# Hybrid decoder trunk: other start addresses for the operands that TensorE reads

## The chip, the cores and the metric

The kernel runs on one core of a Trainium2 chip. The metric is the device time of one execution in microseconds. Before the change the median of 3 runs is 823.48 us (822.98 to 824.05).

## What is computed

The reference is a decoder trunk of two layers over 256 tokens of width 1024, all in float32. A layer is a SwiGLU feed-forward block (width 1408, half a step), a token-mixing block and a second feed-forward block:

```python
for l in range(DEPTH):                                             # DEPTH = 2
    x = x + 0.5 * _swiglu(_rms_norm(x, ffn1_norm[l]), ffn1_wi[l], ffn1_wo[l])
    u = _rms_norm(x, mix_norm[l])
    c = _split_cols(u @ w_in[l] + b_in[l])                         # 1024 x 6312
    y_sb = _stick_breaking_attention(...); y_ml = _mlstm(...); y_mla = _mla(...)
    g = sigmoid(c['gates'])                                        # three gates of 1024
    merged = g0*(y_sb @ w_up_sb[l]) + g1*(y_ml @ w_up_ml[l]) + g2*(y_mla @ w_up_mla[l])
    x = x + merged @ w_out[l]
    x = x + 0.5 * _swiglu(_rms_norm(x, ffn2_norm[l]), ffn2_wi[l], ffn2_wo[l])
```

Nearly all arithmetic is in products of the 256 tokens with weight matrices that stream once from HBM.

## The kernel before

Float32 precision is kept with two numbers of type float32r for each value, a high part and the rest. `mm3` (L604) makes each product of three matmuls: standing high by moving high, standing high by moving low, standing low by moving high. "Standing" is the operand that a weight load (LDWEIGHTS) puts into the array ahead of the matmul, 128 columns of 4 bytes, so 512 bytes of each partition; "moving" is the operand that then streams through, 256 to 512 columns, so 1024 to 2048 bytes. Each matmul has its own weight load, and the load for the next one runs beside the matmul.

In most products the weights stand and the activations move, 256 tokens at a time: the normed input `u` (L613), the hidden rows of the feed-forward blocks and the merged branches, in the buffers R1 to R4. Each k-slice is a row of 256 float32, 1024 bytes. A few products are turned round (`tok_units`, L712; the first columns of the mixing block, L952; the last output projection, L862): there the activations stand and the weights move.

A weight tile lands by DMA in a buffer `raw`; ScalarE makes its high part (`conv_hi`, L364), VectorE the rest (`conv_lo`, L374). The two parts go either into a ring of five buffers each (`whi`, `wlo`) or into two of eight slots of 4 KB (`g4_0` to `g4_7`). The slots also hold the gates and the outputs of the three branches, and these outputs move against `whi` and `wlo` in the up projections (L1092).

Start addresses are set by `LAYOUT` (L210): before anything else the constructor takes these buffers in this order, each group padded to a multiple of 256 bytes. The activations begin 12 floats further (`SHIFT`, L209, in `moving`, L250), and so do weights that move (L366). In the built program this gives, modulo 256 bytes: activations at 48, ring weights that stand at 0, ring weights that move at 48, all slots at 0. Every row and every 128-column piece is a multiple of 256 bytes long, except the 424-column rows, so these numbers hold for each operand. In the text a pair (48, 0) means moving at 48 and the next standing operand at 0.

The order of the work is not fixed by hand: while the program is built, `Flow` (L84) keeps estimated times, and `drive` (L416) issues matmuls, conversions and side work by them. `Flow` notes when a piece of 256 bytes of a tile is written (`pieces`, L109), counted from the start of its tile.

Of the kernel before, what the change touches and what calls it, by code (L numbers as in the profile page):

```python
# [11 lines left out]
F32R = mybir.dt.float32r  # L12
# [6 lines left out]
P = 128  # L19
S = 256  # L20
# [52 lines left out]
class WTile:  # L73


    def __init__(self, srcs, shape, cls):
        self.srcs, self.shape, self.cls = srcs, shape, cls
        self.n = int(np.prod(shape))
        self.first = self.last = self.hi = self.lo = None
        self.not_before = 0  # L80
        self.moves = False
# [121 lines left out]
class Trunk:  # L203
# [2 lines left out]
    SLACK, NEAR, BACK = 0.1, 6, 1.5  # L206


    FIRST, LINE, SHIFT = 16512, 256, 12  # L209
    LAYOUT = (("u", 4112, 1), ("R2", 2064, 1), ("R1", 2072, 1), ("R3", 784, 1), ("R4", 784, 1),  # L210
              ("whi", 1088, 5), ("wlo", 1088, 5), *((f"g4_{i}", 1024, 1) for i in range(8)))

    def __init__(self, ctx, tc, a, out):
        self.tc, self.a, self.out = tc, a, out
        self.nc = Core(tc.nc)
        self.flow = self.nc.flow
        pool = lambda name, **k: ctx.enter_context(tc.tile_pool(name=name, bufs=1, **k))
        self.cp = self.wp = self.ap = pool("all")
        self.mm = pool("mm", space=bass.MemoryType.PSUM)
        self.at = pool("at", space=bass.MemoryType.PSUM)  # L220
        self.n = 0
        self.units, self.tiles, self.hooks = [], [], {}
        self.sides = []
        self.ring = {}
        self.slots = {"ps": [None] * 4, "mm": [None] * 2, "t384": [None] * 6, "g4": [None] * 8}
        self.last = {k: list(v) for k, v in self.slots.items()}
        end = self.FIRST
        for tag, n, bufs in self.LAYOUT:
            pad = -end % self.LINE
            if pad:  # L230
                self.ap.tile([P, pad // 4], F32, tag=f"before_{tag}", name=f"before_{tag}", bufs=1)
            self.tile(self.ap, [P, n], tag, bufs, F32R)
            end += pad + -(-n // 8) * 32 * bufs
# [12 lines left out]

    def sb(self, shape, tag, bufs=1, dt=F32):
        return self.tile(self.ap, shape, tag, bufs, dt)

    def moving(self, shape, tag):  # L250

        n = int(np.prod(shape[1:]))
        t = self.sb([P, self.SHIFT + n], tag, dt=F32R)[:, self.SHIFT:]
        return t.rearrange("p (a b c) -> p a b c", a=shape[1], b=shape[2]) if len(shape) == 4 else t.rearrange("p (a c) -> p a c", a=shape[1])

    def s2k(self, shape):
        return self.sb(shape, "s2k", 5)
# [105 lines left out]

    def conv_hi(self, w):  # L364
        if w.slot == "m":
            o = self.SHIFT if w.moves else 0  # L366
            w.fh, w.fl = (self.tile(self.wp, [P, 1088], s, self.RING, F32R)[:, o:o + 1024] for s in ("whi", "wlo"))
        else:
            w.fh, w.fl = self.g4([P, 1024], F32R), self.g4([P, 1024], F32R)
        view = lambda t: t[:, :w.n].rearrange("p (a b) -> p a b", a=w.shape[0])  # L370
        w.hi, w.lo = view(w.fh), view(w.fl)
        self.nc.scalar.copy(w.fh[:, :w.n], w.raw[:, :w.n])
# [237 lines left out]


    def new_u(self, N):
        u = self.moving([P, 2, 8, S], "u")  # L613
        N["h"], N["l"] = u[:, 0], u[:, 1]
        N["n"] = N["m"] = 0

# [130 lines left out]
    def plan_ffn(self, l, wi, wo, U, N):  # L747
        a, nc = self.a, self.nc
        H = {"k": set()}

        def hT(k):
            if k not in H["k"]:
                return None
            return (H["ah"][:, k], H["al"][:, k]) if k < 8 else (H["bh"][:, k - 8], H["bl"][:, k - 8])

        def alloc():
            if len(H) == 1:
                H["ah"], H["al"] = self.moving([P, 8, S], "R1"), self.moving([P, 8, S], "R2")
                H["bh"], H["bl"] = self.moving([P, 3, S], "R3"), self.moving([P, 3, S], "R4")

        def dst(k0, n):
            hi, lo, k = (H["ah"], H["al"], k0) if k0 < 8 else (H["bh"], H["bl"], k0 - 8)
            H["k"].update(range(k0, k0 + n))
            return hi[:, k:k + n], lo[:, k:k + n]

        wv = a[wi][l].rearrange("(k p) (g f) -> p k g f", p=P, g=2)

        def tiles(c0, w, cuts):
            return [WTile([(wv[:, k0:k1, g, c0:c0 + w], (0, k1 - k0, g * w, (g + 1) * w)) for g in range(2)],
                          (k1 - k0, 2 * w), "mx") for k0, k1 in zip(cuts, cuts[1:])]  # L770

        def side_feat(box, k0, n):
            v = box["v"]
            alloc()
            yield lambda: "row" in U,
            yield "v", U["row"], v
            h = self.s2k([P, 2, 256])[:, :n]
            nc.vector.tensor_tensor(h, v[:, 0:n, :], U["row"].unsqueeze(1).to_broadcast([P, n, S]), ALU.mult)
            yield "a", h
            nc.scalar.activation(h, h, AF.Silu)  # L780
            yield "v", h
            nc.vector.tensor_tensor(h, h, v[:, n:2 * n, :], ALU.mult)
            self.give(box["pp"])
            yield "a", h
            hi, lo = dst(k0, n)
            self.split(hi, lo, h)

        for c in range(5):
            box = {}
            cuts = (0, 1, 2, 4, 6, 8) if not self.units else (0, 2, 4, 6, 8)  # L790
            self.feat_units(tiles(256 * c, 256, cuts), 4, U, box,
                            lambda b=box, c=c: self.spawn(side_feat(b, 2 * c, 2)), key="n")
        box = {}
        self.feat_units(tiles(1280, 128, (0, 4, 8)), 2, U, box, lambda b=box: self.spawn(side_feat(b, 10, 1)), key="n")
        if N is None:
            self.plan_last(a[wo][l], 11, hT, U)
        else:
            self.plan_down(a[wo][l], 11, hT, N, U)
# [124 lines left out]
    def plan_mix(self, l, U, M, N):  # L923
        nc, a = self.nc, self.a
        col = lambda r: M["cols"][:, r:r + 1]
        wv = a["w_in"][l].rearrange("(k p) n -> p k n", p=P)
        b = a["b_in"][l]
# [158 lines left out]
        def up_units(q):  # L1086
# [5 lines left out]
            def part(w, j, k, kk, first, last):  # L1092

                if "p" not in box:
                    pp = self.big_ps()
                    box["p"] = [self.main_ps(), pp[:, 0, :], self.main_ps(), pp]
                y = M["y", j]
                for mi in range(2):
                    ms = slice(mi * P, (mi + 1) * P)
                    self.mm3(box["p"][j][:, mi * S:(mi + 1) * S], w.hi[:, kk, ms], w.lo[:, kk, ms], y[0][:, k], y[1][:, k],  # L1100
                             first, last, first=mi == 0)
                if last:
                    box["j"] = j
                    if j == 0:
                        self.spawn(merge())

            def merge():
                if q == 0:
                    M["mh"], M["ml"] = self.moving([P, 8, S], "R1"), self.moving([P, 8, S], "R2")
                    M["merged"] = 0  # L1110
                acc = None
                m0 = 2 * (q % 2)
                for j in (0, 1, 2):
                    yield lambda: box["j"] >= j,
                    yield "v", M["g", q // 2, j], box["p"][j]
                    o = self.s2k([P, 2, S])
                    nc.vector.scalar_tensor_tensor(o, M["g", q // 2, j][:, m0:m0 + 2, :], 1.0,
                                                   box["p"][j].rearrange("p (m c) -> p m c", m=2), ALU.add, ALU.mult)
                    if acc is None:
                        acc = o  # L1120
                    else:
                        nc.vector.tensor_tensor(acc, acc, o, ALU.add)
                self.give(box["p"][0], *box["p"][2:])
                if q % 2:
                    self.give(*[M["g", q // 2, j] for j in range(3)])
                yield "a", acc
                self.split(M["mh"][:, 2 * q:2 * q + 2], M["ml"][:, 2 * q:2 * q + 2], acc, 0.5)
                M["merged"] += 1
# [400 lines left out]
```

## Time and profile before

| | |
|---|---|
| median of 3 runs | 823.48 us (822.98 to 824.05) |
| profiled execution, its own time | 823.87 us |
| its span, first to last instruction | 822.1 us |
| TensorE busy | 814.6 us, 99% of the span, 6475 matmuls |
| weight loads busy | 788.0 us, 6475 loads |
| VectorE, ScalarE, GpSimd busy | 587.1, 455.4, 35.4 us |
| granted TensorE clock | 1.00 of 2.4 GHz over the span |

Busy time counts a matmul from its start to its modelled end, and matmuls overlap, so a busy share of 99% says that TensorE hardly ever waits, not how fast it goes. How fast it goes is read from starts: in the timeline, the difference between two start times divided by the number of matmuls in between is the interval that one matmul costs. All recorded instructions have line 189, the helper that records them, so groups go by tile names: `u` and `R` are activations, `whi` and `wlo` the ring, `g` the slots, `t` the small 1536-byte buffers. The first name after the arrow moves, the second stands; `at` and `mm` are PSUM buffers.

### The profile page before, as it was taken

The numbers are of one execution on the slowest core, as the hardware profiler recorded it, in microseconds if no ns is written. First come the engines' busy times: TensorE is split into PE (matmuls) and PEld (weight loads), VectorE is DVE, ScalarE is ACT, GpSimd is POOL, SyncE is SP. The second block draws the span as 40 slices with busy tenths as digits, with TensorE's granted clock in tenths as the row PEclk, the third lists the DMA queues.
The fourth block names the chain that finished last, engine by engine and source line by source line (L and its number), as shares of the span: only waits on it lengthen the run. The fifth ranks groups of instructions, "written<-read, shape, count | busy, mean of one in ns | idle before, by whom it ended". The sixth has DMA issues, their size and how long they took to land.

```text
span 822.1 us, 16189 instructions
## 1 busy us (share of the span) xinstructions
PE 814.6 (99%) x6475; PEld 788.0 (96%) x6475; DVE 587.1 (71%) x943; ACT 455.4 (55%) x724; POOL 35.4 (4%) x51
## 2 busy tenths in 40 slices
PE   8999999999999999999999999999999999999998
PEld 6999999899999999999999999998999999999996
DVE  5687878989667488755776567789967585886641
ACT  7456645658675546544554444665576845555430
POOL 0000000200200000000000000110003000000000
PEclk9999999999999999999999999999999999999999
DMA  8678834654264757865576554366543665587611
GB/s 257 197 226 253 266 110 137 202 156 122 85 205 153 233 167 219 258 191 168 155 228 204 179 166 141 105 207 182 157 119 112 200 183 183 179 250 218 185 67 52
DMA packets 122384, 145.41 MB, mean 177 GB/s; under 512 B 7542, under 2 KB 97092, under 8 KB 122308
## 3 DMA queue, kind: packets, MB, share of 16 engines
q1 hardware_dynamic: 122148, 144.30, 57.7%
q8 instruction: 51, 0.84, 0.4%
q14 instruction: 25, 0.20, 0.1%
q10 hardware_dynamic: 160, 0.07, 0.1%
HBM read 143.29 MB, written 1.05 MB: 176 GB/s over the span
## 4 chain that ended last, share of the span: by engine, by line
PE 94%; DMA 2%; ACT 1%; SPq 1%; DVE 1%; issue 0%; POOL 0%; DVEq 0%; ACTq 0%; POOLq 0%
PE mm L189 61%; PE at L189 33%; DMA raw<-in_ffn_wi_dram 2%; SPq L189 1%; ACT g L189 1%; DVE g L189 0%; POOL rstd L189 0%; ACT s2k L189 0%; ACT x L189 0%; ACT whi L189 0%; ACT t L189 0%; DVE s2k L189 0%; ACT u L189 0%; DVE xn L189 0%; DVE t L189 0%
## 5 line engine op out<-in xcount | busy, mean ns | idle before, releaser
L189 PE MATMUL mm<-u,whi 128*128 128x256 f32 x1728 | 312.7, 283 | 0.0
L189 ACT CAST whi<-raw 128x1024 fp32r<-128x1024 f32 (+3 forms) x186 | 190.6, 1032 | 153.9 <-PE mm L189 46.0
L189 PEld LDWEIGHTS mm<-u,whi 128*128 128x128 f32 x1728 | 264.9, 188 | 0.9 <-issue 0.7
L189 DVE TENSOR_TENSOR wlo<-raw,whi 128x1024 fp32r<-128x1024 f32 (+3 forms) x186 | 220.2, 1197 | 57.4 <-ACT whi L189 54.0
L189 PE MATMUL mm<-u,wlo 128*128 128x256 f32 x864 | 242.7, 281 | 0.0
L189 PEld LDWEIGHTS mm<-u,wlo 128*128 128x128 f32 x864 | 162.4, 188 | 0.0
L189 ACT CAST g<-raw 128x1024 fp32r<-128x1024 f32 (+3 forms) x86 | 87.3, 1021 | 79.0 <-PE mm L189 19.7
L189 PE MATMUL mm<-u,g 128*128 128x256 f32 x1056 | 129.3, 281 | 0.7 <-DVE g L189 0.7
L189 PEld LDWEIGHTS mm<-u,g 128*128 128x128 f32 x1056 | 126.6, 188 | 0.9 <-DVE g L189 0.9
L189 DVE TENSOR_TENSOR g<-raw,g 128x1024 fp32r<-128x1024 f32 (+3 forms) x86 | 101.3, 1187 | 28.0 <-ACT g L189 27.5
L189 PE MATMUL at<-R,g 128*128 128x256 f32 x594 | 72.6, 281 | 0.0
L189 PEld LDWEIGHTS at<-R,g 128*128 128x128 f32 x594 | 71.3, 188 | 0.0
L189 PE MATMUL at<-R,whi 128*128 128x256 f32 x388 | 69.5, 281 | 0.0
L189 PEld LDWEIGHTS at<-R,whi 128*128 128x128 f32 x388 | 59.4, 188 | 0.0
L189 PE MATMUL mm<-whi,u 128*128 128x512 f32 (+1 forms) x168 | 56.2, 386 | 0.0
L189 PE MATMUL at<-R,wlo 128*128 128x256 f32 x194 | 54.5, 281 | 0.0
L189 DVE TENSOR_TENSOR R<-s2k,R 128x512 fp32r<-128x512 f32 (+1 forms) x24 | 15.6, 649 | 29.4 <-ACT R L189 29.3
L189 PEld LDWEIGHTS mm<-whi,u 128*128 128x128 f32 x168 | 31.5, 188 | 5.2
L189 PEld LDWEIGHTS at<-R,wlo 128*128 128x128 f32 x194 | 36.5, 188 | 0.0
L189 PE MATMUL mm<-wlo,u 128*128 128x512 f32 (+1 forms) x84 | 32.1, 382 | 0.0
L189 POOL TENSOR_TENSOR rcol<-rcol,mhalf 128x2 f32<-128x2 f32 x6 | 7.0, 1175 | 491.6 <-DVE rcol L189 491.6
L189 ACT ACTIVATE u<-x,cols 128x256 fp32r<-128x256 f32 x40 | 18.2, 501 | 12.6 <-DVE x L189 12.6
(221 smaller groups left out, 995.8 us busy)
## 6 DMA issues: line engine op xcount, KB each, us to landing
raw<-in_w_in_dram SPq DMA_DIRECT2D x92, 512.0 KB
raw<-in_ffn_wi_dram SPq DMA_DIRECT2D x174, 256.0 KB
raw<-in_ffn_wo_dram SPq DMA_DIRECT2D x35, 512.0 KB
raw<-in_w_out_dram SPq DMA_DIRECT2D x16, 512.0 KB
raw<-in_ffn_wo_dram SPq DMA_DIRECT2D x12, 384.0 KB
raw<-in_w_up_ml_dram SPq DMA_DIRECT2D x16, 256.0 KB
raw<-in_w_in_dram SPq DMA_DIRECT2D x8, 424.0 KB
raw<-in_w_up_sb_dram SPq DMA_DIRECT2D x8, 256.0 KB
```

The source lines that it names most:

```text
L189: f(*args, **kw)
```

## The change

The activations now begin at the start of their padded buffers, at 0 modulo 256. A ring buffer begins at 192; weights that stand begin 4 floats into it (`STAND`), at 208, and weights that move 16 floats into it (`MOVE`), at 0 of the next 256 bytes. The slots begin at 224. So the pairs become: activations against standing ring weights (48, 0) to (0, 208); activations against standing slots (48, 0) to (0, 224); branch outputs against standing ring weights (0, 0) to (224, 208); moving ring weights against standing activations (48, 48) to (0, 0); moving slots against standing activations (0, 48) to (224, 0).

```diff
-    FIRST, LINE, SHIFT = 16512, 256, 12
-    LAYOUT = (("u", 4112, 1), ("R2", 2064, 1), ("R1", 2072, 1), ("R3", 784, 1), ("R4", 784, 1),
-              ("whi", 1088, 5), ("wlo", 1088, 5), *((f"g4_{i}", 1024, 1) for i in range(8)))
+    FIRST, LINE, STAND, MOVE = 16512, 256, 4, 16
+    LAYOUT = (("u", 4096, 1, 0), ("R2", 2048, 1, 0), ("R1", 2072, 1, 0), ("R3", 768, 1, 0), ("R4", 768, 1, 0),
+              ("whi", 1088, 5, 192), ("wlo", 1088, 5, 192), *((f"g4_{i}", 1024, 1, 224) for i in range(8)))
...
-        for tag, n, bufs in self.LAYOUT:
-            pad = -end % self.LINE
+        for tag, n, bufs, at in self.LAYOUT:
+            pad = (at - end) % self.LINE
...
-    def moving(self, shape, tag):
-
-        n = int(np.prod(shape[1:]))
-        t = self.sb([P, self.SHIFT + n], tag, dt=F32R)[:, self.SHIFT:]
-        return t.rearrange("p (a b c) -> p a b c", a=shape[1], b=shape[2]) if len(shape) == 4 else t.rearrange("p (a c) -> p a c", a=shape[1])
...
-            o = self.SHIFT if w.moves else 0
+            o = self.MOVE if w.moves else self.STAND
...
-        u = self.moving([P, 2, 8, S], "u")
+        u = self.sb([P, 2, 8, S], "u", dt=F32R)
...
-                H["ah"], H["al"] = self.moving([P, 8, S], "R1"), self.moving([P, 8, S], "R2")
-                H["bh"], H["bl"] = self.moving([P, 3, S], "R3"), self.moving([P, 3, S], "R4")
+                H["ah"], H["al"] = self.sb([P, 8, S], "R1", dt=F32R), self.sb([P, 8, S], "R2", dt=F32R)
+                H["bh"], H["bl"] = self.sb([P, 3, S], "R3", dt=F32R), self.sb([P, 3, S], "R4", dt=F32R)
```

(`merge`, L1109, changes in the same way as `alloc`.) No operation is added or removed. But the rows of the activations now share no 256-byte piece with their neighbours, so `Flow` believes some of them ready at another time, and the order shifts in places.

The first place is TensorE in the first chunk of layer 0's second feed-forward block; `at<-consts,sq` is the column sum of squares for the norm. Before:

```order
L189 MATMUL mm_615_4047<-u_3874,whi_3928 128x256 x2
L189 MATMUL mm_615_4047<-u_3874,wlo_3929 128x256
L189 MATMUL at_623_4112<-consts_87,sq_3906 128x1 x2
L189 MATMUL mm_615_4047<-u_3874,whi_3928 128x256 x2
L189 MATMUL mm_615_4047<-u_3874,wlo_3929 128x256
L189 MATMUL mm_615_4047<-u_3874,whi_3928 128x256 x2
L189 MATMUL mm_615_4047<-u_3874,wlo_3929 128x256
L189 MATMUL mm_615_4047<-u_3874,g_1_604_3962 128x256 x2
```

and now:

```order
L189 MATMUL mm_615_4045<-u_3872,whi_3922 128x256 x2
L189 MATMUL mm_615_4045<-u_3872,wlo_3923 128x256
L189 MATMUL mm_615_4045<-u_3872,g_1_604_3967 128x256 x2
L189 MATMUL mm_615_4045<-u_3872,g_2_605_3968 128x256
L189 MATMUL mm_615_4045<-u_3872,g_1_604_3967 128x256 x2
L189 MATMUL mm_615_4045<-u_3872,g_2_605_3968 128x256
L189 MATMUL at_622_4118<-consts_85,sq_3904 128x1 x2
L189 MATMUL mm_615_4045<-u_3872,g_1_604_3967 128x256 x2
```

The sum moved 12 matmuls later.

The second place is TensorE in the first columns of layer 1's mixing block, where weights move against `u`; before:

```order
L189 MATMUL at_905_6337<-whi_6115,u_6124 128x256
L189 MATMUL mm_903_6330<-whi_6186,u_6124 128x424
L189 MATMUL mm_903_6330<-wlo_6187,u_6124 128x424
L189 MATMUL mm_903_6330<-whi_6186,u_6124 128x424
L189 MATMUL at_905_6337<-g_1_893_6220,u_6124 128x256
L189 MATMUL at_905_6337<-g_2_894_6221,u_6124 128x256
L189 MATMUL at_905_6337<-g_1_893_6220,u_6124 128x256
```

and now:

```order
L189 MATMUL at_908_6341<-whi_6113,u_6122 128x256
L189 MATMUL mm_907_6337<-g_1_890_6184,u_6122 128x424
L189 MATMUL mm_907_6337<-g_2_891_6185,u_6122 128x424
L189 MATMUL mm_907_6337<-g_1_890_6184,u_6122 128x424
L189 MATMUL at_908_6341<-whi_6221,u_6122 128x256
L189 MATMUL at_908_6341<-wlo_6222,u_6122 128x256
L189 MATMUL at_908_6341<-whi_6221,u_6122 128x256
```

The same products stand in the same order, but the wide tile came into slots and the narrow one into the ring.

## Rows read from the trace of the kernel before

**Rows 1.** The page: busy time by engine, granted clock in slices, chain by engine.

```profile
PE 814.6 (99%) x6475; PEld 788.0 (96%) x6475; DVE 587.1 (71%) x943; ACT 455.4 (55%) x724; POOL 35.4 (4%) x51
...
PEclk9999999999999999999999999999999999999999
...
PE 94%; DMA 2%; ACT 1%; SPq 1%; DVE 1%; issue 0%; POOL 0%; DVEq 0%; ACTq 0%; POOLq 0%
```

**Rows 2.** Waits of PE: waiting <- waited for: us in total, times, longest.

```profile
PE at L189 <- DMA R<-in_x_dram: 1.1, 2, 0.7
```

**Rows 3.** Chain in order of time, a long piece: start us, us, what, matmuls.

```profile
68.08 36.92 PE at L189 x312
```

**Rows 4.** Groups by form on PE: names, shapes, count, busy us, mean ns, idle.

```profile
L189 PE MATMUL mm<-u,whi 128*128 128x256 f32 x1728 | 312.7, 283 | 0.0
L189 PE MATMUL mm<-u,wlo 128*128 128x256 f32 x864 | 242.7, 281 | 0.0
L189 PE MATMUL mm<-u,g 128*128 128x256 f32 x1056 | 129.3, 281 | 0.7 <-DVE g L189 0.7
L189 PE MATMUL at<-R,g 128*128 128x256 f32 x594 | 72.6, 281 | 0.0
L189 PE MATMUL at<-R,whi 128*128 128x256 f32 x388 | 69.5, 281 | 0.0
L189 PE MATMUL at<-R,wlo 128*128 128x256 f32 x194 | 54.5, 281 | 0.0
...
L189 PE MATMUL mm<-whi,u 128*128 128x512 f32 x128 | 42.1, 397 | 0.0
...
L189 PE MATMUL mm<-g,whi 128*128 128x256 f32 x128 | 23.4, 283 | 0.0
...
L189 PE MATMUL at<-u,g 128*128 128x256 f32 x144 | 17.7, 281 | 0.0
```

**Rows 5.** Timeline of PE, up projection, (0, 0): start us, us, instruction, count.

```profile
251.51 0.40 PE L189 MATMUL mm<-g,whi 128*128 128x256 f32 x2
...
254.39 0.40 PE L189 MATMUL at<-g,whi 128*128 128x256 f32 x2
```

**Rows 6.** Timeline of PE, 512 moving columns, (48, 48): first and last of 25.

```profile
157.85 0.39 PE L189 MATMUL mm<-wlo,u 128*128 128x512 f32 x1
...
163.38 0.39 PE L189 MATMUL mm<-wlo,u 128*128 128x512 f32 x1
```

**Rows 7.** Timeline of PE, last projection: starts of four tiles, 15 matmuls each.

```profile
790.12 1.56 PE L189 MATMUL mm<-g,R 128*128 128x512 f32 x6
...
792.92 0.40 PE L189 MATMUL mm<-whi,R 128*128 128x512 f32 x1
...
795.71 0.39 PE L189 MATMUL mm<-whi,R 128*128 128x512 f32 x1
...
798.47 0.39 PE L189 MATMUL mm<-whi,R 128*128 128x512 f32 x1
```

**Rows 8.** Timeline of PE, latent up projections of both layers, moving at 0.

```profile
143.77 0.34 PE L189 MATMUL at<-whi,t 128*128 128x384 f32 x1
...
144.65 0.56 PE L189 MATMUL at<-whi,t 128*128 128x384 f32 x2
145.05 0.39 PE L189 MATMUL at<-wlo,t 128*128 128x512 f32 x1
145.28 0.57 PE L189 MATMUL at<-whi,t 128*128 128x512 f32 x2
...
550.23 0.40 PE L189 MATMUL at<-wlo,t 128*128 128x512 f32 x1
550.47 0.39 PE L189 MATMUL at<-whi,t 128*128 128x512 f32 x1
550.70 0.39 PE L189 MATMUL mm<-whi,u 128*128 128x512 f32 x1
```

More of the change, by code (lines that the diff above doesn't have):

```diff
@@ L1108, in merge @@
                 if q == 0:
-                    M["mh"], M["ml"] = self.moving([P, 8, S], "R1"), self.moving([P, 8, S], "R2")
+                    M["mh"], M["ml"] = self.sb([P, 8, S], "R1", dt=F32R), self.sb([P, 8, S], "R2", dt=F32R)
                     M["merged"] = 0
```

## The prediction

> **What bounds the kernel now.** I read the page first. TensorE is busy for 814.6 us of the span of 822.1, the chain that ended last is TensorE for 94%, and the granted clock is full, 2.4 GHz, in every slice [rows 1]. The list of PE's waits comes next: its longest entry is 1.1 us in total [rows 2], and the groups show an idle time of 0.0 for the big products [rows 4]. So no other engine is waited for after the first microseconds, and the time is the number of matmuls times the interval from one start to the next. That interval is read in the chain and the timeline. In the last stage of a feed-forward block 312 matmuls of 256 columns take 36.92 us, 118.3 ns each [rows 3]. At the granted clock 256 columns are 106.7 ns, so 11.6 ns of each interval are something else. The change touches nothing but addresses, so the question is how much of these 11.6 ns depends on them.
>
> The trace has four pairs of addresses to compare (moving, next standing, modulo 256).
> - (48, 0), activations against standing weights: 118.3 ns [rows 3].
> - (0, 0), the branch outputs, which lie in slots, against standing ring weights: eight groups of three matmuls from 251.51 to 254.39, 2.88 us over 24, so 120.0 ns [rows 5].
> - (48, 48), weights that move against activations: 24 matmuls of 512 columns in 5.53 us, 230.4 ns each [rows 6]. In the last projection a ring tile takes nine matmuls of 512 columns and six of 256; two tiles in a row take 5.55 us, 2.775 each, which leaves (2775 - 9 x 230.4) / 6 = 116.9 ns for 256 columns [rows 7].
> - (0, 48), the same with the tile in a slot: 2.80 us for the 15 matmuls, 25 ns more, or 1.7 ns for each [rows 7]; about 118.6 ns for 256 columns.
>
> Two things follow. First, addresses matter, in steps of about 1.7 ns, between 116.9 and 120.0. Second, the 256 further columns of a 512-column matmul, beside which no new weight load has to run, cost 230.4 - 116.9 = 113.5 ns and not 106.7: 6.8 ns more for 1024 bytes, 1.7 ns for each 256 bytes. The step has the size of one such piece.
>
> **The change part by part.** Counts are from the groups [rows 4].
>
> Activations against standing ring weights, 1728 + 864 + 388 + 194 = 3174 matmuls, go from (48, 0) to (0, 208). This is the term that decides, and no row shows (0, 208). The distance from standing to moving stays at 48, so what the two reads do to each other by distance stays as it is. A row of 1024 bytes that begins at 48 lies in five pieces of 256 bytes and one that begins at 0 in four; if each piece costs the 1.7 ns above, the interval falls to 116.6, and 116.9 is an interval that the trace does show. Bounds: 116.5 below, the lowest 256-column equivalent that I find; above, 120.0 from (0, 0), and 121.5 from the dearest rows of the latent projections, where moving is at 0 as well. There the standing operands lie at 32, 160 and 224: five matmuls of 384 columns from 143.77 to 144.65 are 176.0 ns each, or 119.3 less the further columns; one of 512 columns from 145.05 to 145.28 is 230 ns, equal to 116.5 for 256; two from 550.23 to 550.70 are 235 each, equal to 121.5 [rows 8]. So moving at 0 is not dear in itself: it reaches the lowest interval with some standing addresses and the highest with others. I take 116.6, a step lower, because the distance that gave 118.3 is kept: 3174 x -1.7 = -5.4 us. The whole range is 3174 x -1.8 = -5.7 to 3174 x 3.2 = +10.2.
>
> Activations against standing slots, 1056 + 594 + 144 = 1794 matmuls, go from (48, 0) to (0, 224), a distance of 32 and not 48. The latent rows hold that very pair for a third of their matmuls, with 116.5, 119.3 and 121.5 for their stretches [rows 8]. I take 118.8, between the first two: 1794 x 0.5 = +0.9 us, with bounds of -3.2 and +5.7.
>
> Branch outputs against standing ring weights, 128 in the row shown and 128, 64 and 64 in its sisters, 384 in all, go from (0, 0) to (224, 208). The nearest pairs are the 120.0 that they have now and the 116.9 of (48, 48), where neither lies at 0. The middle, 118.4, gives 384 x -1.6 = -0.6 us, bounds -1.2 and +0.6.
>
> Weights that move from the ring go from (48, 48) to (0, 0): 192 matmuls of 512 columns against `u` (128 and half as many low parts), about 60 more of that width in the last projection, about 110 of 256 columns. With 120.0 for 256 columns and the middle of 230 and 235 for 512 this is 252 x 2.1 + 110 x 3.1 = +0.9 us, bounds 0 and +1.6. Weights that move from slots, some 165, go from (0, 48) to (224, 0); both have one operand at 0, and I leave them.
>
> The order moves a little. The sum of squares of layer 0's second feed-forward block stands 12 matmuls later, 1.4 us. What hangs on it is the release of the first chunk's PSUM, which TensorE needs two chunks on; the second chunk, 96 matmuls or 11.4 us, hides it, and without that cover it would cost the 1.4 us once. Which tile comes into a slot and which into the ring changes here and there, as for the wide tiles of layer 1's first columns, but the totals hardly do. Conversions write and read as many bytes as before on ScalarE and VectorE, which have 45% and 29% of the span free [rows 1]. Cost: nothing.
>
> Sum: -5.4 + 0.9 - 0.6 + 0.9 = -4.2 us on the profiled execution's 823.87, so 819.7. That execution is 0.4 above the median of the runs, which gives 819.3.
>
> **A rule that speaks against it.** The interval at (0, 0) is 1.7 ns above that at (48, 0), with the same shapes and the same weights' buffers [rows 3, 5]. The Trainium skill, page "TensorE: Matmul & The Clock Gate", section "Step-by-step: what each phase is for", says that TensorE has two independent read ports, one for the moving operand and one for the weight load, and that loading the next weights takes no read bandwidth from the running matmul. By that rule the standing address could do nothing to the matmul beside it and the sum would be about 0, so 823.5. The trace disagrees, by 120.0 against 118.3. The same page, section "Back-to-back issue gap", gives N / 2.4 + 2.5 ns for a matmul alone, an estimate of 109.2 ns for 256 columns; the trace has 116.5 at its lowest, so I don't count on a gain beyond that.
>
> **The rivals.**
> - The two moves cancel (0.25). Read as a table, standing at 48 and not at 0 saves 1.4 ns (120.0 to 118.6) and moving at 48 and not at 0 saves 1.7 (both with standing at 0 and at 48). If 208 is to the standing operand what 48 is, (0, 208) is like (0, 48), 118.6, and the ring term is +1.0 us and the slot term +0.5; with the other two +1.8, so 825.3, and 823 to 827 by the bounds of the smaller ones. For it: it uses all four pairs. Against it: (48, 48) and (0, 0) have the same distance, so the table has to leave distance out, while rows 8 show three intervals at one moving address.
> - Moving at 0 costs a step whatever stands (0.21). Then both big groups run at the 120.0 of rows 5: (3174 + 1794) x 1.7 = +8.4, and with the other terms +8.7: 832.2. The place is the feed-forward and mixing products, the price 1.7 ns for each matmul. It decides as soon as the ring's interval stays above 118.0, where the loss of the other terms eats its gain. For it: (0, 0) and (0, 48) are each dearer than their neighbours at 48. Against it: the 230 ns of rows 8 with moving at 0.
> - Slots fall too (0.10). If (0, 224) also reaches 116.6, the slot term is -3.0 and the sum -8.1: 815.4; with every term at its lower bound 813.
> - The change does nothing that can be measured, since the reads don't meet (0.03): 823.5. Rows 3 and 5 speak against it.
> - A new wait by the changed order (0.03): every few late sums cost 1.4 us, 825 to 829. The zero idle of rows 4 speaks against it.
>
> **How the numbers follow.** My forecast, ring down a step, has 0.38 and a range of its own of 816 to 821.5. About 0.2%, 1.6 us, is what a measurement of this kernel can tell from no change. Faster is the forecast, the deeper case and 0.02 of the cancelling one: 0.50. Same is 0.11 of the cancelling case, whose middle lies close to that bound, and the 0.03 without effect: 0.14. Slower is 0.12 of the cancelling case, 0.21 and 0.03: 0.36. The range from 812.5 to 830 holds the deeper case, the forecast, the cancelling case and about half of the slower one, which ends a little beyond it.
>
> **What would show it.** In the changed profile the piece of 312 matmuls tells the main term: 36.4 us if the ring and slot intervals average 116.6, 36.9 if nothing happened, 37.4 if moving at 0 costs a step. Ring and slots must be read apart there, in stretches of the timeline with `whi` and with `g` alone. Branch outputs must show less than 2.88 us for eight groups, and the 24 matmuls of 512 columns more than 5.53. PE's idle time must stay at a few microseconds; if it grows, the order is to blame. The forecast is wrong if the ring's interval is not below 118.0.

## The result and the profile after

The changed kernel takes 814.43 us (median of 4 runs, 813.61 to 816.03) against 823.39 us (822.98 to 824.05, 4 runs): ratio 0.9893, 95% interval 0.9876 to 0.9910. That is 9.0 us, where the forecast had 4.2; the two profiled executions, 823.87 and 814.13 us, lie 9.7 apart. The page, to be held against [rows 1]:

```profile
span 812.3 us, 16199 instructions
...
PE 805.5 (99%) x6475; PEld 779.9 (96%) x6475; DVE 586.7 (72%) x943; ACT 455.4 (56%) x724; POOL 32.7 (4%) x51
...
PEclk9999999999999999999999999999999999999999
```

As many matmuls at the same clock, 9.1 us less busy time on TensorE; VectorE and ScalarE are as before. The list of PE's waits (waiting <- waited for: us, times, longest) says that no new wait came: the first line stands in the list of the kernel before with the same 1.1 us, the second with 0.7 [rows 4], the third with 1.1 [rows 2].

```profile
PE mm L189 <- POOL mhalf L189: 1.1, 1, 1.1
PE mm L189 <- DVE g L189: 0.8, 1, 0.8
PE at L189 <- DMA R<-in_x_dram: 0.6, 1, 0.6
```

The groups by form, with the mean duration of one matmul behind the busy time; in [rows 4] these means were 283, 281 and 281:

```profile
L189 PE MATMUL mm<-u,whi 128*128 128x256 f32 x1680 | 300.7, 280 | 0.0
...
L189 PE MATMUL mm<-u,g 128*128 128x256 f32 x1128 | 137.6, 280 | 0.8 <-DVE g L189 0.8
...
L189 PE MATMUL at<-R,g 128*128 128x256 f32 x570 | 69.1, 279 | 0.0
```

The chain has the 312 matmuls of [rows 3] again, now 116.7 ns each, and a piece of 144 in layer 0's mixing block, in which only ring weights stand, 116.7 as well:

```profile
67.17 36.40 PE at L189 x312
125.44 16.81 PE mm L189 x144
```

The timeline gives the rest (start, duration, instruction, count). First 72 matmuls with standing slots from 58.61 to 67.01, 116.7 ns. Then branch outputs, eight groups of three: in the first quarter of the output columns 250.42 to 253.30, still the 2.88 us of [rows 5]; in the third quarter 282.87 to 285.69, 2.82 us. Last, 21 matmuls of 512 columns from 156.74 to 161.50, 226.7 ns, where [rows 6] have 230.4.

```profile
58.61 8.56 PE L189 MATMUL mm<-u,g 128*128 128x256 f32 x72
67.01 2.96 PE L189 MATMUL at<-u,g 128*128 128x256 f32 x24
...
156.74 0.39 PE L189 MATMUL mm<-wlo,u 128*128 128x512 f32 x1
...
161.50 0.39 PE L189 MATMUL mm<-wlo,u 128*128 128x512 f32 x1
...
250.42 0.40 PE L189 MATMUL mm<-g,whi 128*128 128x256 f32 x2
...
253.30 0.40 PE L189 MATMUL at<-g,whi 128*128 128x256 f32 x2
...
282.87 0.40 PE L189 MATMUL mm<-g,whi 128*128 128x256 f32 x2
...
285.69 0.39 PE L189 MATMUL at<-g,whi 128*128 128x256 f32 x2
```

Giving each matmul of the trace its two addresses from the built program, and taking start to start, the means over all of a pair are: (0, 208) 116.70 ns, (0, 224) 116.74, (224, 208) 118.59, moving ring weights (0, 0) 227.72 for 512 columns and 117.79 for 256. The 118.59 is a mean of two values: 119.9 in the first half of the output columns and 117.3 in the second, 96 matmuls each, in both layers alike. Intervals in which TensorE waited are left out. The intervals below are read in this way where a table or a count stands beside them.

### The profile page after: what moved, and what is told of

Same layout as the page of the kernel before. It is cut to its first block, busy times and chain, and to the rows that moved or that the text cites. A ratio compares the mean times of both kernels' runs of the same rounds, so it can differ in the third digit from the quotient of the medians.

```text
span 812.3 us, 16199 instructions
## 1 busy us (share of the span) xinstructions
PE 805.5 (99%) x6475; PEld 779.9 (96%) x6475; DVE 586.7 (72%) x943; ACT 455.4 (56%) x724; POOL 32.7 (4%) x51
## 4 chain that ended last, share of the span: by engine, by line
PE 95%; DMA 2%; ACT 1%; DVE 1%; issue 0%; SPq 0%; POOL 0%; DVEq 0%; ACTq 0%; POOLq 0%
PE mm L189 62%; PE at L189 33%; DMA raw<-in_ffn_wi_dram 2%; DMA mg<-in_ml_out_norm_dram 1%; DVE g L189 0%; ACT g L189 0%; SPq L189 0%; ACT s2k L189 0%; ACT x L189 0%; DVE s2k L189 0%; ACT u L189 0%; DVE xn L189 0%; POOL s2k L189 0%; DVE u L189 0%; DVE gain L189 0%
## 5 line engine op out<-in xcount | busy, mean ns | idle before, releaser
L189 PE MATMUL mm<-u,whi 128*128 128x256 f32 x1680 | 300.7, 280 | 0.0
L189 PEld LDWEIGHTS mm<-u,whi 128*128 128x128 f32 x1680 | 256.1, 188 | 0.7 <-issue 0.5
L189 PE MATMUL mm<-u,wlo 128*128 128x256 f32 x840 | 233.5, 278 | 0.0
L189 PEld LDWEIGHTS mm<-u,wlo 128*128 128x128 f32 x840 | 157.6, 188 | 0.0
L189 PE MATMUL mm<-u,g 128*128 128x256 f32 x1128 | 137.6, 280 | 0.8 <-DVE g L189 0.8
L189 PEld LDWEIGHTS mm<-u,g 128*128 128x128 f32 x1128 | 134.1, 188 | 1.1 <-DVE g L189 1.0
L189 PE MATMUL at<-R,g 128*128 128x256 f32 x570 | 69.1, 279 | 0.0
L189 PEld LDWEIGHTS at<-R,g 128*128 128x128 f32 x570 | 67.7, 188 | 0.0
L189 PE MATMUL mm<-whi,u 128*128 128x512 f32 (+1 forms) x152 | 49.3, 387 | 0.0
L189 DVE SCALAR_TENSOR_TENSOR u<-x,cols,u 128x256 fp32r<-128x256 f32 x40 | 17.6, 481 | 10.3 <-ACT u L189 10.3
```

Of the source, the lines that this page charges most:

```text
L189: f(*args, **kw)
```

## The experiments

Theory at the start, from the prediction: an interval is the number of 256-byte pieces of the moving row plus a part that goes by the distance from standing to moving. Rivals: the standing address alone decides; a few pairs are good and no simple rule holds.

**Three sweeps of the standing address**, with the activations at 0, at 48 and at 64 (`u`; the hidden rows elsewhere in the last two).

```diff
+    OFFS = (20, 28, 36, 52, 60)
...
-              ("whi", 1088, 5, 192), ("wlo", 1088, 5, 192), *((f"g4_{i}", 1024, 1, 224) for i in range(8)))
+              ("whi", 1088, 5, 192), ("wlo", 1088, 5, 192), *((f"g4_{i}", 1024, 1, at) for i, at in enumerate((0, 32, 64, 96, 128, 160, 192, 224))))
...
-            o = self.MOVE if w.moves else self.STAND
+            o = self.OFFS[len(self.ring["whi"]) % 5]
```

`OFFS` has the floats by which the five ring buffers' operands begin later; the other sweeps have other lists there and in `LAYOUT`.

> Activations move at 0 as in the changed kernel, but the standing addresses are spread: the ring's buffers at 16, 48, 80, 144 and 176, the eight slots at 0, 32, ... 224 (modulo 256). Read by address from the trace, so one run gives the interval of 256 columns at (0, s) for thirteen s. Theory of pieces and distance: moving at 0 is four pieces, so 116.7 ns for every s except where the standing piece lies at the moving one's own address; (0, 0) 120.0, the others 116.6 to 117. Rival, standing table: 0 alone is dear, because it was dear against 48 too (118.3), and all the others are cheap: the same picture here, told apart in the next two runs. Rival, a few good addresses: only 208 and 224 are cheap, 48 and 160 (seen dear in the latent products) give 118.5 to 120. Time: 814 to 816 by the first two, 818 to 821 by the third.

> The same sweep with the inputs u moving at 48 and the hidden rows at 80, 112, 208 and 240; ring at 16, 48, 112, 144, 208, slots at 0, 32, ... 224. Pieces and distance: a row that begins anywhere but at 0 lies in five pieces, so every interval is a step of 1.7 ns above that of the same distance at moving 0: most 118.3, none below 118.0, (48, 48) and the like 120 to 121.7; time 821 to 825. Standing table: the standing address alone decides, so (48, 48), (48, 112) and (48, 208) are 116.7 as at moving 0, and only standing 0 gives 118.3 or more; time 814 to 817. Distance alone: the interval at (48, s) equals that at (0, s - 48).

> The same sweep with u moving at 64, R2 at 128, R1 at 160, the rest at 0; ring at 16, 48, 80, 112, 208, slots at 0, 32, ... 224. Pieces of 256 bytes: 64, 128 and 160 are not multiples of 256, so each interval is a step above the one at moving 0: 118.3 and more; time 821 to 824. If the pieces are of 64 bytes, 64 and 128 are as good as 0: 116.7, and 160 (an odd multiple of 32) is a step above. Standing table: 116.7 for all standing addresses that were cheap in the run at moving 0.

Measured: 824.31, 820.21 and 822.52 us (one run each; the kernel before 823.7 on that chip). Intervals in ns of 256 columns against standing ring weights, up to 24 in a row at one address, some 490 to 650 matmuls for each value:

| moving | standing at 16 | 48 | 80 | 112 | 144 | 176 | 208 |
|---|---|---|---|---|---|---|---|
| 0 | 118.4 | 117.9 | 118.7 | | 119.2 | 118.1 | |
| 48 | 118.3 | 117.9 | | 114.5 | 116.9 | | 119.4 |
| 64 | 117.0 | 118.2 | 118.4 | 117.8 | | | 119.5 |

The 117.9 at (0, 48) leaves out 34 intervals of 130 ns, nearly all of them every second one in three of its tiles; with them it is 118.5. All expectations by a rule fail: moving at 0 is dear with five standing addresses out of five, 208 is cheap with moving at 0 (116.7 in the changed kernel) and the dearest at 48 and 64, and rows at 48 and 64, in five pieces, reach 114.5 and 117.0. The rival of a few good addresses comes nearest, though the first sweep's time lies above its 818 to 821. The cheapest value stands in the timeline of the second sweep, a ring tile at 112 of 24 matmuls in 2.74 us, 114.2 each:

```profile
56.45 0.40 PE L189 MATMUL mm<-u,whi 128*128 128x256 f32 x2
...
59.19 0.52 PE L189 MATMUL mm<-u,g 128*128 128x256 f32 x3
```

The slots lay at eight addresses, two by turns in a product, and the price there is not the one of the pair alone: (0, 224) has 117.8 against 116.7 in the changed kernel, (48, 224) 117.8 against 119.8 in a run below.

**Slots back at 0.**

```diff
-              ("whi", 1088, 5, 192), ("wlo", 1088, 5, 192), *((f"g4_{i}", 1024, 1, 224) for i in range(8)))
+              ("whi", 1088, 5, 192), ("wlo", 1088, 5, 192), *((f"g4_{i}", 1024, 1, 0) for i in range(8)))
```

> The changed kernel with the slots put back at 0, so activations against standing slots are (0, 0) in place of (0, 224), the branch outputs (0, 208) in place of (224, 208). Distance: the slots' interval rises from 116.7 to 120.0, 1794 x 3.3 = +5.9 us, less 0.7 us on the branch outputs, so 819.6. If with moving at 0 it doesn't matter where the slots lie: 814. Forecast's reading of the old pair (0, 0) is right only in the first case.

819.08 us (5 runs), near the expected 819.6; ratio 0.9940 (0.9927 to 0.9954). Ratios here and below are to the kernel before, run beside it on the same chip: 823.7 us in this group, 824.0 and 824.4 in the later ones. The chain's piece with ring weights stays, the 72 matmuls with slots go from 8.40 to 8.63 us, 119.9 ns:

```profile
69.29 36.89 PE at L189 x312
128.03 16.80 PE mm L189 x144
```

```profile
60.49 8.79 PE L189 MATMUL mm<-u,g 128*128 128x256 f32 x72
69.12 3.04 PE L189 MATMUL at<-u,g 128*128 128x256 f32 x24
```

So where the slots lie is worth about half of the 9.0 us, once the activations are at 0.

**Standing ring weights back at 0.**

```diff
-    FIRST, LINE, STAND, MOVE = 16512, 256, 4, 16
+    FIRST, LINE, STAND, MOVE = 16512, 256, 16, 16
```

> The changed kernel with the standing ring weights put back at 0: (0, 208) becomes (0, 0) for 3174 matmuls, (224, 208) becomes (224, 0) for the branch outputs; slots and moving weights as changed. If moving at 0 is dear only against standing at 0: 116.7 to 119.7 ns, 3174 x 3.0 = +9.5 us on 814.4, so 824. If the whole gain is the start of the activations in four pieces and the standing address does nothing: 814.4.

823.74 us (10 runs), ratio 1.000 (0.999 to 1.0009). The piece with ring weights takes 17.27 us, 119.9 ns:

```profile
67.22 36.91 PE at L189 x312
126.14 17.27 PE mm L189 x144
```

One constant, which moves only the standing operand, takes back the whole gain. The weight load itself, as recorded, is longer too: the ring's takes 188 ns on average before the change and in the changed kernel, and 191 here, where the slots' stays at 188. Before, changed, and this run (mean ns behind the busy time):

```profile
L189 PEld LDWEIGHTS mm<-u,whi 128*128 128x128 f32 x1728 | 264.9, 188 | 0.9 <-issue 0.7
L189 PEld LDWEIGHTS mm<-u,whi 128*128 128x128 f32 x1680 | 256.1, 188 | 0.7 <-issue 0.5
L189 PEld LDWEIGHTS mm<-u,whi 128*128 128x128 f32 x1680 | 261.6, 191 | 0.7 <-issue 0.5
```

At (48, 0), the first line, the standing operand lies at 0 as well, so the longer load comes with the pair (0, 0). The Trainium skill, page "TensorE: Matmul & The Clock Gate", section "Step-by-step: what each phase is for", gives the weight load a read port of its own and says that it takes no read bandwidth from the matmul beside it. The trace speaks against two reads that don't touch each other: the interval goes from 116.7 to 119.9 ns and the load from 188 to 191. Which of the two reads holds up the other, no run shows.

**All addresses 64 bytes later.**

```diff
-    LAYOUT = (("u", 4096, 1, 0), ("R2", 2048, 1, 0), ("R1", 2072, 1, 0), ("R3", 768, 1, 0), ("R4", 768, 1, 0),
-              ("whi", 1088, 5, 192), ("wlo", 1088, 5, 192), *((f"g4_{i}", 1024, 1, 224) for i in range(8)))
+    LAYOUT = (("u", 4096, 1, 64), ("R2", 2048, 1, 64), ("R1", 2072, 1, 64), ("R3", 768, 1, 64), ("R4", 768, 1, 64),
+              ("whi", 1088, 5, 0), ("wlo", 1088, 5, 0), *((f"g4_{i}", 1024, 1, 32) for i in range(8)))
```

> Every address of the changed kernel 64 bytes later (activations 64, standing ring 16, slots 32, moving ring 64), all distances kept. Forecast's pieces: a row at 64 lies in five pieces of 256 bytes, a step of 1.7 ns for 4968 matmuls, +8.4 us: 822.9. Distance, with a frame that repeats every 64 bytes: (64, 16) and (64, 32) are 116.7 as (0, 208) and (0, 224), 814.4. The sweep's 117.0 for (64, 16), between other tiles, speaks for the second.

813.87 us (4 runs), ratio 0.9884 (0.9867 to 0.9900), and the same pieces to a hundredth:

```profile
67.01 36.40 PE at L189 x312
125.28 16.81 PE mm L189 x144
```

This is the 814.4 that was expected if only distance and a frame of 64 bytes count. A row at 64 lies in five pieces of 256 bytes and costs what a row at 0 costs. The forecast's pieces fall. A shift by 64 changes nothing; one by 48 does, since (48, 0) and (0, 208) have one distance and 118.3 and 116.7 ns.

**The slots' part alone, in the kernel before** (with one scratch buffer of 2 KB less, for room).

```diff
-            pad = -end % self.LINE
+            pad = (224 * tag.startswith("g4") - end) % self.LINE
...
-        return self.sb(shape, "s2k", 5)
+        return self.sb(shape, "s2k", 4)
```

> The kernel before with one part of the change alone, the slots at 224 (activations at 48, ring at 0; four scratch buffers for room): slots (48, 0) to (48, 224), branch outputs (0, 0) to (224, 0). If the start of the standing operand has a value of its own: 116.7 for 1832 matmuls, -2.9 us, and -0.6 for the branch outputs, 820. If only the pair counts, the second sweep's (48, 224), 117.8 among other addresses, -0.9 and -0.6: 822. Distance in another frame, 48 against 32: 118.3, 823.4.

826.29 us (10 runs), 0.3% slower: ratio 1.0026 (1.0016 to 1.0035). None of the three expected times came. The ring's piece is 17.04 us, 118.3 ns; with slots 72 matmuls take 8.63 us, 119.9 ns:

```profile
127.62 17.04 PE mm L189 x144
```

```profile
59.74 8.79 PE L189 MATMUL mm<-u,g 128*128 128x256 f32 x72
68.37 3.04 PE L189 MATMUL at<-u,g 128*128 128x256 f32 x24
```

The same 224 saves 3 ns with the activations at 0 and costs 1.5 with them at 48. No address is good or bad by itself, and the parts of the change don't add up one by one. Moving ring weights have (48, 48) here as in the kernel before, but their 24 matmuls of 512 columns take 5.60 us, 233.3 ns, and not the 5.53 us of [rows 6]. So the two addresses modulo 256 don't fix the interval alone; no run shows what else does.

```profile
157.31 0.40 PE L189 MATMUL mm<-wlo,u 128*128 128x512 f32 x1
...
162.91 0.40 PE L189 MATMUL mm<-wlo,u 128*128 128x512 f32 x1
```

**Moving ring weights back at 48.**

```diff
-    FIRST, LINE, STAND, MOVE = 16512, 256, 4, 16
+    FIRST, LINE, STAND, MOVE = 16512, 256, 4, 28
```

> The changed kernel with only the ring weights that move put back at 48 (standing activations stay at 0): 512 columns (0, 0) to (48, 0), 256 columns likewise. The forecast gave the change of this part +0.9 us, the trace after showed 227.7 in place of 230.4 ns, -0.7. If the pair decides: 231.3 as in the first sweep, 236 x 3.6 = +0.85, and 0.1 for 256 columns, so 815.4. If what it did before, (48, 48), is the same at any distance: 230.4, +0.6. If moving at 0 is the dear one, as forecast: 813.5.

816.36 us (4 runs), ratio 0.9914 (0.9880 to 0.9948). The interval overlaps that of the changed kernel, so the time decides nothing; the trace does, 24 matmuls of 512 columns in 5.60 us, 233.3 ns, against 226.7:

```profile
157.14 0.40 PE L189 MATMUL mm<-wlo,u 128*128 128x512 f32 x1
...
162.74 0.40 PE L189 MATMUL mm<-wlo,u 128*128 128x512 f32 x1
```

Moving at 0 was the cheaper one here, against the forecast.

**Activations at 48, ring at 112.**

```diff
-    FIRST, LINE, SHIFT = 16512, 256, 12
+    FIRST, LINE, SHIFT, STAND, MOVE = 16512, 256, 4, 4, 4
+    LAYOUT = (("u", 4104, 1, 32), ("R2", 2056, 1, 32), ("R1", 2072, 1, 32), ("R3", 776, 1, 32), ("R4", 776, 1, 32),
+              ("whi", 1088, 5, 96), ("wlo", 1088, 5, 96), *((f"g4_{i}", 1024, 1, 128) for i in range(8)))
...
+            pad = (at - end) % self.LINE
...
+            o = self.MOVE if w.moves else self.STAND
```

> Activations at 48 as in the kernel before, standing and moving ring weights at 112, slots at 128. In the second sweep (48, 112) stood at 113.9 to 114.5 ns, below the lowest of the kernel before. If that is the pair's own: 3174 x -2.5 = -7.9 us on 814.4, the slots at 116.7 to 118.8 (0 to +3.7), so 806 to 810. If it came from the other addresses around it, an interval goes back to a multiple of the step, 115.0 or 116.7: 809 to 818. Pieces: five for each row, no interval below 118: 821 or more.

810.96 us (4 runs), ratio 0.9846 (0.9832 to 0.9861): the ring at 113.9 ns over 3141 matmuls, as expected of the pair, the slots, at 128, at 119.3 over 1779, above the 118.8 of the expectation, and so the time above its 806 to 810. In the chain:

```profile
125.72 16.37 PE mm L189 x144
```

**Activations at 0, all else at 64, twice.**

```diff
-    FIRST, LINE, STAND, MOVE = 16512, 256, 4, 16
+    FIRST, LINE, STAND, MOVE = 16512, 256, 0, 0
...
-              ("whi", 1088, 5, 192), ("wlo", 1088, 5, 192), *((f"g4_{i}", 1024, 1, 224) for i in range(8)))
+              ("whi", 1088, 5, 64), ("wlo", 1088, 5, 64), *((f"g4_{i}", 1024, 1, 64) for i in range(8)))
```

> Activations at 0, ring weights (standing and moving) and slots all at 64: the distance of (48, 112), 48 bytes lower. If distance alone decides: 114 ns for 4957 matmuls, -13 us on 814.4, so 801. If the place of the moving row within 64 bytes matters too, the first sweep's 118.3 for (0, 64): +7.9, so 822.

> The kernel with activations at 0 and all else at 64, once more. There 2464 stretches of 13 matmuls ran at 113.3 ns and 1817 at 118.3, in long pieces that begin and end at short matmuls of other kinds. If the program and its addresses decide which, the same pieces come again at the same places and the time is 810. If both values are steady and chance (arrival of data at the interruptions) decides, the pieces lie elsewhere and their shares differ: 804 to 814.

808.92 us (4 runs, 806.47 to 810.12), ratio 0.9817 (0.9798 to 0.9836); again, 808.99 (one run). Neither expected interval came: the mean over 4908 matmuls is 115.3 ns. The chains of the two executions show why, the first run's and then the second's:

```profile
68.29 36.75 PE at L189 x312
126.79 16.96 PE mm L189 x144
...
372.07 35.36 PE at L189 x312
```

```profile
68.64 36.75 PE at L189 x312
127.14 16.34 PE mm L189 x144
...
371.42 35.36 PE at L189 x312
```

The same 312 matmuls take 36.75 us in layer 0's first block and 35.36 at 372, 117.8 and 113.3 ns. The piece of 144 ran at 117.8 ns in one execution and at 113.5 in the other, of one program. So one pair has two steady intervals, 113.3 and 117.8 (the expectation of the second run calls the upper one 118.3; over every long stretch it is 117.8); stretches of up to 760 matmuls stay in one, and the change comes at interruptions, a wait or short matmuls of another kind. In the second execution most pieces were as in the first and three stretches, 33 to 41, 127 to 143 and 721 to 731 us, were not: neither the program alone nor chance alone decides.

**Activations at 48, ring and slots at 112**, which the last two layouts point to; the edit beside that of "Activations at 48, ring at 112":

```diff
+              ("whi", 1088, 5, 96), ("wlo", 1088, 5, 96), *((f"g4_{i}", 1032, 1, 96) for i in range(8)))
...
-        return self.sb(shape, "s2k", 5)
+        return self.sb(shape, "s2k", 4)
...
-        return self.take("g4", shape, dt)
+        t = self.take("g4", [P, 4 + 1024], dt)[:, 4:]
...
```

> Activations at 48 and everything else at 112, the slots too (they get 4 floats more; to make room the pool of 2 KB scratch tiles has four buffers in place of five). The pair (48, 112) gave 113.9 ns over 3141 matmuls with the ring alone. Theory, the pair's own interval: 4959 matmuls at 113.9 against the 116.7 of the changed kernel, -14 us, so about 800, and TensorE waits no more than before. Rival, the interval has more than one steady value for a pair and another mix of tiles falls into another: some stretches at 116.7 or 118.3, 804 to 812. Rival, the missing scratch buffer stalls VectorE and TensorE after it: the interval 113.9, but idle time on TensorE of several microseconds.

801.27 us (4 runs), ratio 0.9722 (0.9708 to 0.9737) to the kernel before; against the changed kernel's 0.9893 another 1.7%. (48, 112) is 113.6 ns over 4906 matmuls; its stretches of 22 and more lie between 113.3 and 114.9, with no second value such as 117.8. Timeline, 72 matmuls in 8.16 us, and waits:

```profile
60.42 8.32 PE L189 MATMUL mm<-u,g 128*128 128x256 f32 x72
68.58 2.88 PE L189 MATMUL at<-u,g 128*128 128x256 f32 x24
```

```profile
PE at L189 <- DMA R<-in_x_dram: 2.1, 3, 0.9
PE mm L189 <- DVE g L189: 1.1, 2, 0.8
...
PE mm L189 <- DVE wlo L189: 0.7, 1, 0.7
```

The rival of several microseconds of stalls came in small part at most: the waits of the list sum to 5.5 us, against 2.8 in the changed kernel. Of the difference 1.5 us is for the first input, and 0.7 is a wait for a low part from VectorE that the list of the changed kernel does not have. Whether that one comes from the missing scratch buffer or from TensorE's shorter intervals isn't shown.

## Why the prediction was right in sign and half the size

- **What bounds the kernel** was right: addresses alone moved the time, and the intervals account for it. By the forecast's counts: ring 3174 x -1.63 = -5.2 us, slots 1794 x -1.6 = -2.9, branch outputs 384 x -1.3 = -0.5, moving ring weights 252 x -2.7 and 110 x +0.9 = -0.6: about -9.1, measured -9.0. Two counts are off in the forecast, neither by enough to matter: the built program has 3222 matmuls against the ring, which is 0.1 us, and 135, not 165, in which slots move. That last part, left at nothing, stayed: 232.9 and 233.0 ns for 512 columns.
- **The ring's term** was right in its number, 116.6 forecast and 116.7 measured, and wrong in its reason, so the number came out by luck. Five pieces against four is refuted by the shift by 64, and a kept distance doesn't keep the interval. The second half of the 512-column matmul, from which the piece was made, is no proof of a price by pieces.
- **The slots' term** is the step that failed: "I take 118.8, between the first two", +0.9 us; measured 116.7 and -2.9, which is 3.8 of the 4.8 us missing. One of the two values that it was put between, 116.5, is a single interval from a timeline that shows 10 ns, six of the steps in question, and [rows 8] hold (0, 224) only in turn with standing operands at 32 and 160. The first sweep shows that such company changes the price: 117.8 there, 116.7 where the pair repeats. The rival "slots fall too", at 0.10 and 815.4, is what happened.
- **The moving ring weights** failed in sign, +0.9 forecast, -0.6 measured. That is about 1.4 us more, and the ring and the branch outputs, each a little smaller than forecast, take 0.3 back. The (0, 0) of the branch outputs was carried to weights that move, and they run at 117.8, not at 120.0.
- **The branch outputs** came out in the sum, -0.5 for -0.6, but the check named for them, less than 2.88 us for eight groups, failed in the first half of the columns, with 2.88 still, and held in the second, with 2.82.
- **The order** cost nothing, as forecast; the list of waits has 1.1 us at most.
- **The rivals.** "Moving at 0 costs a step whatever stands" fell, with 116.7 in both big groups, though with other neighbours moving at 0 did stay above that: 117.9 to 119.2 in the first sweep. "The two moves cancel" read 208 as 48; (0, 48) is 117.9 or, with its long intervals, 118.5, and (0, 208) 116.7. "Does nothing" fell with the ring put back at 0.

Open stays why a pair has its interval. The runs show no rule in distance, in pieces or in the standing address, and of the frame they show only that a shift by 64 leaves it as it is and one by 48 doesn't. Branch outputs bear the first out: 119.9 at (0, 0) in the kernel before and at (64, 64) with all else at 64. Only addresses modulo 256 were looked at, and pairs with two values are left unexplained too. Other places for (48, 112)'s distance than 48 and 0 were not tried.

## What to carry to other kernels

When matmuls follow each other without waits, compare their start-to-start intervals between stretches whose operands begin at different addresses: here 113.6 to 119.9 ns for one shape, and the best layout tried took 2.8% off the whole time. Measure the exact pair, repeated, with the two operands moved together; the price of one part alone, or of a pair among other pairs, had the wrong sign or size. Sweep first and choose then, and look whether an interval has one steady value.

## What was not expected of the hardware

Where one pair repeats, long stretches of 256 columns hold one interval: 113.3, 116.7, 117.3, 117.8, 118.3, 119.3 or 119.9 ns. The pair modulo 256 doesn't always say which: (0, 64) has 113.3 and 117.8, branch outputs at (224, 208) have 119.9 and 117.3, and 512 columns at (48, 48) 230.0 in the kernel before and 233.2 with the slots alone moved, over 71 matmuls each. The lowest steady interval seen for 256 columns, 113.3 ns, is 6.6 above the 106.7 that the prediction gives the columns at the full clock. The Trainium skill, page "TensorE: Matmul & The Clock Gate", section "Back-to-back issue gap", gives N / 2.4 + 2.5 ns for a single matmul without the weight load, an estimate of 109.2 for 256 columns; here, where each matmul has a load, no steady stretch reached it.
